# Six attention heads with three dilations: one masked key row per query against a near and a far part

## The chip, the cores and the metric

The program runs on one NeuronCore of a Trainium2 chip. The metric is the device time of one execution in microseconds (us); the median of three executions stands for the kernel. The engines are TensorE (PE, with its weight loads as PEld), VectorE (DVE), ScalarE (ACT), GpSimd (POOL) and SyncE (SP), which issues the DMAs.

## The reference, cut to what matters

A trunk of two layers over 1024 tokens of width 1024, in float32. Each layer is one input projection, three token mixers side by side (retention, dilated attention, spatial gating), an output projection and a SwiGLU. The change touches only the attention of six heads of width 64:

```python
DILATED_PATTERNS = ((128, 1), (512, 4), (2048, 16))
# each pattern: causal attention to t, t-d, ..., t-window; output o and log-denominator lse
w = jax.nn.softmax(jnp.stack(lses, axis=0), axis=0)
return jnp.sum(w[..., None] * jnp.stack(outs, axis=0), axis=0)
```

Mixing the three patterns by their log-denominators is the same as one softmax in which a key that stands in two or three patterns counts two or three times. A query thus sees every key up to 128 tokens back and, farther back, only keys at a distance that is a multiple of 4.

## The kernel before

All matrices are held as two float32r parts (high and low), so that a product is two or three matmuls. A Python scheduler writes the program: coroutines for the attention units, projections and weight loads are advanced against an estimated clock, and `Program.order` then lists the operations of each engine by start in that estimate. On the chip every engine works through its list in order. Copies may be given to ACT or DVE, whichever the scheduler finds freer. DMAs all go through SP's queue in its listed order; a DMA waits there for what it reads and for its semaphore's earlier use.

Buffers come from pools of slots: `U` (128x1024 floats in SBUF, 44), `H` (128x512, 10), `ST` (small statistics, 24), `B` (the 8 PSUM banks).

Attention of one layer: 6 heads, each as 4 units of 256 queries (`att_unit(head, j)`), on 4 lanes that interleave with the projections of gating and retention. A unit makes `qd` (queries high and low), then for each of its two tiles of 128 queries the scores against all earlier keys (`sb_b<-ks_u,qd_h`, up to 1024 columns, high and low), one DVE pass that adds the mask and takes the row maximum (shown as CUSTOM_DVE, in an order as ISA), an exponential on ACT with the row sum, a reciprocal, and a scaling of the whole row (`pr_u<-pr_u,st_st`). PE then transposes the row by blocks of 128 (`tb_b<-cst,pr_u`), ACT or DVE split the transposed block into `ph`/`pl`, and PE multiplies by the values (`ob_b<-ph_h,vs_u`, 256 queries wide). The mask holds the log of the count of patterns:

```python
dist = (NT - 1) * P + i[:, None] - np.arange(S)[None, :]
...
mm(ob[:, i0 * P:256], vs[:, k, :], hi[:, pos:pos + w], k == 0, False)
```

Of the kernel before, what the change touches and what calls it, by code (L numbers as in the profile page):

```python
# [18 lines left out]
P = 128  # L19
# [55 lines left out]
def _constants():  # L75
    c = np.zeros((P, K_END), np.float32)
    i = np.arange(P)
    c[:, K_ID:K_ID + P] = np.eye(P)
    c[:, K_TRIL:K_TRIL + P] = i[:, None] >= i[None, :]
    lg = np.log(1.0 - 2.0 ** (-5.0 - np.arange(6)))  # L80
    diff = (i[None, :] - i[:, None]).astype(np.float64)
    for h in range(6):
        c[:, K_DEC + h * P:K_DEC + (h + 1) * P] = np.where(
            diff >= 0, np.exp(-lg[h] * (i[:, None] + 1.0)) * HD ** -0.5, 0.0)
        c[:, K_ZETA + h] = np.exp(lg[h] * (P - 1.0 - i)) * HD ** -0.5
    for p in range(3):
# [7 lines left out]
    dist = (NT - 1) * P + i[:, None] - np.arange(S)[None, :]  # L94
    count = np.zeros(dist.shape)
    for window, dil in ((128, 1), (512, 4), (2048, 16)):
        count += (dist >= 0) & (dist <= window) & (dist % dil == 0)
    with np.errstate(divide="ignore"):
        mask = np.where(count > 0, HD ** 0.5 * np.log(count), NEG)
    return c, mask.astype(np.float32)  # L100


class Ref:
# [28 lines left out]
    def rearrange(self, pattern, **kw):  # L132

        left, right = (_axes(x)[1:] for x in pattern.split("->"))
        sizes = dict(kw)
        for group, n in zip(left, self.free.shape):
            known = math.prod(sizes[x] for x in group if x in sizes)
            for x in group:
                sizes.setdefault(x, n // known)
        assert sum(left, []) == sum(right, [])  # L140
        return self._with(("rearrange", (pattern,), kw),
                          free=self.free.reshape([math.prod(sizes[x] for x in g) for g in right]))

# [331 lines left out]
def _body(ctx, tc, nc, x, positions, g_mix_pre, g_mix_post, w_in, w_s, b_s, w_out,  # L475
# [9 lines left out]
    U = Slots(u_pool, "u", 44, [P, 1024])  # L485
    H = Slots(u_pool, "h", 10, [P, 512])
    ST = Slots(u_pool, "st", 24, [P, 8])
    O = Slots(u_pool, "o", 2, [P, 256])
# [18 lines left out]
    rvs = fixed([S, 384], "rvs", pool=dram)  # L507
    gs = fixed([HID, S], "gs", pool=dram)
# [756 lines left out]
    def rope_evac(r, hf, b):  # L1265
        z = H.alloc(name="z")
# [14 lines left out]
    att_left = [0]  # L1281

    def att_pair(p, rq, rk, av):

        pair = [8]
        for e in range(2):
            while U.left < 2 + 2:
                yield None
            a, o = slice(e * HD, e * HD + HD), slice(HD - e * HD, 2 * HD - e * HD)
            ks = U.alloc(dtype=F32R, name="ks")  # L1290
            copy(ks[a], rk[a])
            tt(ks[o], rk[a], ks[a].bitcast(F32), ALU.subtract)
            vs = U.alloc([P, NT, P], F32R, "vs")
            copy(vs[:, :, 0:HD], av[:, :, a])
            tt(vs[:, :, HD:P], av[:, :, a], vs[:, :, 0:HD].bitcast(F32), ALU.subtract)
            head = dict(pair=pair, rq=rq, ks=ks, vs=vs, left=4, p=p, e=e)
            for j in range(4):
                att_q.append((head, j))
            yield ()
        U.free(rk, av)  # L1300

    def att_unit(head, j):
# [5 lines left out]
        while H.left < 3:  # L1308
            yield None
        qd = H.alloc([P, 2, 256], F32R, "qd")  # L1310
        rj = rq[a, j * 256:j * 256 + 256]
        copy(qd[a, 0, :], rj)
        copy(qd[o, 0, :], rj)
        tt(qd[a, 1, :], rj, qd[a, 0, :].bitcast(F32), ALU.subtract)
        copy(qd[o, 1, :], qd[a, 1, :].bitcast(F32))
        yield (qd[:],)
        while U.left < (2 if 3 + p in yT else 3):
            yield None
        if 3 + p not in yT:
            yT[3 + p] = U.alloc(name="yT")  # L1320
            y_left[3 + p] = 8
        pr = [U.alloc(name="pr"), U.alloc(name="pr")]
        for i in range(2):
            t = 2 * j + i
            n = (t + 1) * P
            off = (NT - 1 - t) * P
            st = ST.alloc(name="st")
            nch = (n + 511) // 512
            while B.left < nch + 1:
                yield None  # L1330

            cut = [0, n] if nch == 1 else [0, min(512, n - 256), n]
            for c in range(nch):
                c0, c1 = cut[c:c + 2]
                b = B.alloc(name="sb")
                for v in range(2):
                    mm(b[:, 0:c1 - c0], qd[:, v, i * P:(i + 1) * P], ks[:, c0:c1], v == 0, v == 1)
                sm, mx, ms = pr[i][:, c0:c1], st[:, c:c + 1], L["mask"][:, off + c0:off + c1]
                prog.add(dict(dve=(1.042 * (c1 - c0) + 80, nc.vector.tensor_tensor_reduce)),
                         [sm, mx], [b[:, 0:c1 - c0], ms], out=sm, in0=b[:, 0:c1 - c0], in1=ms, scale=1.0,  # L1340
                         scalar=-3.0e38, op0=ALU.add, op1=ALU.max, accum_out=mx)
                B.free(b)
            if nch == 2:
                tt(st[:, 0:1], st[:, 0:1], st[:, 1:2], ALU.max)
            ts(st[:, 2:3], st[:, 0:1], -HD ** -0.5, ALU.mult)
            act(pr[i][:, 0:n], pr[i][:, 0:n], AF.Exp, scale=HD ** -0.5, bias=st[:, 2:3], accum_out=st[:, 3:4])
            prog.add(dict(dve=(75.0, nc.vector.reciprocal)), [st[:, 4:5]], [st[:, 3:4]],
                     out=st[:, 4:5], in_=st[:, 3:4])
            scaled(pr[i][:, 0:n], pr[i][:, 0:n], st[:, 4:5])
            ST.free(st)  # L1350
            yield ()
        H.free(qd)
        yield (pr[0][:], pr[1][:])
        while B.left < 4 or H.left < 3:
            yield None
        ob = B.alloc(name="ob")
        pend = None
        nb = 2 * j + 2
        for g in range(j + 2):
            new = None  # L1360
            if g <= j:
                while B.left < 2 or H.left < 3:
                    yield None
                b = B.alloc(name="tb")
                pos, lay = 0, []
                for k in (2 * g, 2 * g + 1):
                    i0 = 0 if k <= 2 * j else 1
                    for i in range(i0, 2):
                        tr(b[:, pos + (i - i0) * P:pos + (i - i0 + 1) * P], pr[i][:, k * P:(k + 1) * P])
                    lay.append((k, i0, pos))  # L1370
                    pos += (2 - i0) * P
                hi = H.alloc(dtype=F32R, name="ph")
                lo = H.alloc(dtype=F32R, name="pl")
                copy(hi[:, 0:pos], b[:, 0:pos])
                tt(lo[:, 0:pos], b[:, 0:pos], hi[:, 0:pos].bitcast(F32), ALU.subtract)
                B.free(b)
                new = (hi, lo, lay)
            if pend is not None:
                hi, lo, lay = pend
                for k, i0, pos in lay:  # L1380
                    w = (2 - i0) * P
                    mm(ob[:, i0 * P:256], vs[:, k, :], hi[:, pos:pos + w], k == 0, False)
                    mm(ob[:, i0 * P:256], vs[:, k, :], lo[:, pos:pos + w], False, k == nb - 1)
# [4 lines left out]
        U.free(*pr)  # L1388
        tmp = O.alloc(name="ot")
        y = yT[3 + p]  # L1390
        copy(tmp[0:HD, :], ob[HD:P, 0:256])
        tt(y[a, j * 256:j * 256 + 256], ob[0:HD, 0:256], tmp[0:HD, :], ALU.add)
        B.free(ob)
        O.free(tmp)
        head["left"] -= 1
        head["pair"][0] -= 1
        if head["left"] == 0:
            U.free(ks, vs)
# [13 lines left out]
    def gnorm(src, dst):  # L1412
# [3 lines left out]
        reduce(st[:], src)  # L1416
        ts(st[:], st[:], -1.0 / HD, ALU.mult)
        tt(dst, src, st[:].unsqueeze(2).to_broadcast([P, 8, HD]), ALU.add)
        act(sq[:], dst, AF.Square)
        reduce(st[:], sq[:])  # L1420
        rstd(st[:], HD, 8)
        tt(dst, dst, st[:].unsqueeze(2).to_broadcast([P, 8, HD]), ALU.mult)
# [149 lines left out]
    def layer(l):  # L1572
# [5 lines left out]
        room(3)  # L1578
        av = [U.alloc([P, NT, P], F32, "av") for _ in range(3)]

        def ev_a(t, b):
            for p in range(3):
                copy(av[p][:, t, :], b[:, p * P:(p + 1) * P])
# [15 lines left out]
        dma(L["mask"][:], amask)  # L1599
        sch.spawn(load_ws(l))  # L1600
        att_left[0] = 24
        for _ in range(LANES):
            sch.spawn(att_lane())
        for p in range(3):
# [5 lines left out]
            sch.spawn(att_pair(p, r[0], r[1], av[p]), r[1][:])  # L1610
# [5 lines left out]
        def ev_g(t, b):  # L1616
            for q in range(2):
                act(vg[q][:, t, :], b[:, q * P:(q + 1) * P], AF.Gelu_apprx_tanh)
            if t % 4 == 3:
                for q in range(2):  # L1620
# [13 lines left out]
        def ev_r(t, b):  # L1634
            v = H.alloc([P, 384], F32, "v")
# [125 lines left out]
    if VERBOSE:  # L1761
        print("slots left at the tightest:", {s.tag: s.low for s in (U, H, ST, B, O)},
# [24 lines left out]
```

## Time and profile before

| | |
|---|---|
| time, median of 3 runs | 2313.69 us (2310.02 to 2316.12) |
| profiled execution | 2311.72 us, of which span 2309.9 us |
| PE, PEld busy | 2280.2 us (99%), 1930.3 us (84%) |
| DVE, ACT, POOL busy | 1772.0 us (77%), 886.4 us (38%), 83.1 us (4%) |
| DMA | 225.61 MB, mean 98 GB/s |
| mean granted clock of TensorE | 0.998 of full speed |

The busy time of PE counts each matmul from its start to a modelled end, and matmuls overlap; what a matmul costs the stream is read from the start of one to the start of the next. Attention stands in the profile between about 97 and 322 us and, for the second layer, between about 1239 and 1464 us.

### The profile page before, as it was taken

The page shows a single profiled execution, that of the slowest core. Times are in us where ns is not written, and L with a number is a line of the kernel's source. Part 1 is how long each engine was busy: PE and PEld are TensorE (multiplying, and loading weights), DVE is VectorE, ACT ScalarE, POOL GpSimd, SP SyncE. Part 2 cuts the span into 40 slices and gives each one's busy share as a digit, 9 for nine tenths or more (in the row PEclk, how much of TensorE's full clock was granted, in tenths as well). Part 3 has the DMA queues.
Part 4 walks back from the last instruction along what each step waited for, and adds up shares of the span by engine and source line. Part 5 has one row for each costly group of instructions (what it writes and reads, how often), then busy time and mean ns, then how long its engine had stood idle before and what let it go on. Part 6 is the DMA issues. An engine that isn't in the chain of part 4 may idle for free. (4 is left out here: it accounts for less than half of the span.)

```text
span 2309.9 us, 30253 instructions
## 1 busy us (share of the span) xinstructions
PE 2280.2 (99%) x11320; PEld 1930.3 (84%) x11320; DVE 1772.0 (77%) x3265; ACT 886.4 (38%) x1625; POOL 83.1 (4%) x95
## 2 busy tenths in 40 slices
PE   8999999999999999999999999999999999999998
PEld 7898988887888888878898898888878888888786
DVE  7698876688985554889957898766989755549896
ACT  5367532344122222434344674221632222225441
POOL 1000001010000000000100100000100000000000
PEclk9999999999999999999999999999999999999999
DMA  6211132242432223422342112231623322253142
GB/s 192 78 40 37 58 83 69 96 144 76 133 105 86 84 85 124 177 106 75 132 150 60 32 44 74 77 92 55 193 76 114 101 83 82 82 181 148 55 134 94
DMA packets 213058, 225.61 MB, mean 98 GB/s; under 512 B 14000, under 2 KB 170800, under 8 KB 212912
## 3 DMA queue, kind: packets, MB, share of 16 engines
q1 hardware_dynamic: 212912, 223.69, 30.9%
q8 instruction: 89, 1.46, 0.3%
q14 instruction: 57, 0.47, 0.1%
HBM read 167.01 MB, written 44.04 MB: 91 GB/s over the span
## 5 line engine op out<-in xcount | busy, mean ns | idle before, releaser
L583 PE MATMUL w_b<-hs_u,wh_u 128*128 128x512 f32 x1280 | 394.9, 390 | 2.3 <-DVE wh_u L1760 1.9
L583 PE MATMUL db_b<-wb_u,ga_u 128*128 128x512 f32 x1512 | 347.0, 391 | 2.9 <-DVE ga_u L543 2.6
L583 PE MATMUL fb_b<-hT_u,wh_u 128*128 128x512 f32 x1088 | 344.4, 397 | 0.0
L583 PEld LDWEIGHTS db_b<-wb_u,ga_u 128*128 128x128 f32 x1512 | 284.5, 188 | 65.1 <-DVE ga_u L543 4.1
L583 PEld LDWEIGHTS w_b<-hs_u,wh_u 128*128 128x128 f32 x1280 | 239.7, 188 | 54.2 <-DVE wh_u L1760 2.7
L583 PE MATMUL w_b<-hT_u,wh_u 128*128 128x512 f32 x832 | 257.6, 390 | 0.0
L583 PE MATMUL w_b<-hs_u,wl_u 128*128 128x512 f32 x640 | 248.8, 390 | 1.1 <-DVE wl_u L543 1.1
L583 PEld LDWEIGHTS fb_b<-hT_u,wh_u 128*128 128x128 f32 x1088 | 196.9, 188 | 36.5 <-issue 1.0
L583 PE MATMUL fb_b<-hT_u,wl_u 128*128 128x512 f32 x544 | 212.9, 391 | 0.0
L543 DVE TENSOR_TENSOR c_h<-w_b,c_h 128x512 f32<-128x512 f32 x192 | 131.4, 687 | 80.5 <-PE w_b L583 79.0
L583 PE MATMUL pb_b<-wh_u,hT_u 128*128 128x384 f32 (+1 forms) x768 | 191.0, 324 | 0.0
L543 DVE TENSOR_TENSOR f_u<-f_u,db_b 128x512 f32<-128x512 f32 x232 | 152.2, 684 | 46.7 <-PE db_b L583 46.5
L583 PEld LDWEIGHTS w_b<-hT_u,wh_u 128*128 128x128 f32 x832 | 155.7, 188 | 32.0
L583 PE MATMUL w_b<-hT_u,wl_u 128*128 128x512 f32 x416 | 161.6, 389 | 0.0
L543 DVE TENSOR_TENSOR wl_u<-wr_u,wh_u 128x1024 fp32r<-128x1024 f32 (+1 forms) x130 | 152.6, 1186 | 1.4 <-ACT wh_u L532 0.9
L583 PEld LDWEIGHTS w_b<-hs_u,wl_u 128*128 128x128 f32 x640 | 120.1, 188 | 27.5 <-DVE wl_u L543 2.5
L583 PEld LDWEIGHTS pb_b<-wh_u,hT_u 128*128 128x128 f32 x768 | 134.6, 190 | 1.4 <-ACT hT_u L532 0.3
L583 PE MATMUL pb_b<-wl_u,hT_u 128*128 128x384 f32 (+1 forms) x384 | 122.6, 319 | 0.3 <-DVE wl_u L543 0.3
L583 PEld LDWEIGHTS fb_b<-hT_u,wl_u 128*128 128x128 f32 x544 | 102.1, 188 | 21.8
L532 ACT ACTIVATE wh_u<-wr_u 128x1024 fp32r<-128x1024 f32 (+1 forms) x83 | 84.8, 1037 | 81.8 <-DVE ws_u L543 54.9
L532 ACT ACTIVATE c_h<-w_b 128x512 f32<-128x512 f32 x82 | 49.1, 599 | 165.1 <-PE w_b L583 165.1
L543 DVE TENSOR_TENSOR wl_u<-ws_u,wh_u 128x1024 fp32r<-128x1024 f32 x88 | 106.8, 1217 | 0.1
(198 smaller groups left out, 4059.3 us busy)
## 6 DMA issues: line engine op xcount, KB each, us to landing
wr_u<-w_gate_up SPq DMA_DIRECT2D x176, 256.0 KB, 3.8
gs<-c_h SPq DMA_DIRECT2D x88, 256.0 KB, 2.3
wr_u<-gs SPq DMA_DIRECT2D x44, 512.0 KB, 7.0
wr_u<-w_down SPq DMA_DIRECT2D x44, 512.0 KB, 5.5
wr_u<-w_in SPq DMA_DIRECT2D x38, 512.0 KB, 4.4
sw_h<-z_h SPq DMA_DIRECT2D x192, 64.0 KB, 2.0
wr_u<-w_out SPq DMA_DIRECT2D x16, 512.0 KB, 3.8
wr_u<-w_gate_up SPq DMA_DIRECT2D x16, 512.0 KB, 4.8
```

Of the source, the lines that this page charges most:

```text
L532: alts = dict(act=(act_cost(o, a), lambda out, in_: nc.scalar.activation(out=out, in_=in_, func=AF.Copy)), dve=(1.042 * o.size + 68 if a.r ...
L543: lambda out, in0, in1: nc.vector.tensor_tensor(out=out, in0=in0, in1=in1, op=op))
L583: prog.add(dict(pe=(cost + 3, lambda out, lhsT, rhs: nc.tensor.matmul(out, lhsT, rhs, start=start, stop=stop, skip_group_check=on_top))), ...
```

## The change

A unit is now 512 queries of a head (`att_unit(head, h)`, 2 per head). Its keys are in two parts. The near part: each tile of 128 queries against its own and the previous 128 keys. The far part: queries are regrouped by token mod 4, and each of the 4 groups of 128 queries meets the keys of the same residue, 128 (h = 0) or 256 (h = 1) of them, with keys that the near part has masked out. For that, queries and keys are read with a step of 4 tokens by TensorE. Each part has its own maximum and sum, per query, in different partitions; each part stores them to a DRAM tensor `exch` and loads the other's, and `att_factors` makes the scale from both. Values are stored to DRAM once (`avs`) and loaded in both token orders. The near part's transposed blocks are regrouped by residue as they are split, so that both parts add up in one PSUM bank `ob`. The DMA scratch of the program is set to 1024 bytes, and `U` has 47 slots, `H` 11; `ST` has 20 of twice the width.

```diff
+    dist = P + i[:, None] - np.arange(2 * P)[None, :]
+    dist = np.concatenate([np.where(dist <= P, dist, -1), np.where(4 * dist > P, 4 * dist, -1)], 1)
...
+    def att_factors(x):
+        y = ST.alloc(name="sf")
+        xv = x[:].rearrange("p (w k c) -> p w k c", w=2, k=2)
+        e = y[:, 4:12].rearrange("p (w c) -> p w c", w=2)
+        tt(y[:, 0:4], x[:, 0:4], x[:, 8:12], ALU.max)
+        tt(e, xv[:, :, 0], y[:, 0:4].unsqueeze(1).to_broadcast([P, 2, 4]), ALU.subtract)
+        act(y[:, 4:12], y[:, 4:12], AF.Exp, scale=HD ** -0.5)
+        tt(xv[:, :, 1], xv[:, :, 1], e, ALU.mult)
+        tt(y[:, 0:4], x[:, 4:8], x[:, 12:16], ALU.add)
...
+        tt(y[:, 12:16], y[:, 4:8], y[:, 0:4], ALU.mult)
...
+                if part == 0:
+                    t = 4 * h + c
+                    n = 256 if t else P
+                    ql = [q[:, c * P:(c + 1) * P] for q in (q_hi, q_lo)]
+                    kr = ks[:, (t + 1) * P - n:(t + 1) * P]
...
+                else:
+                    n = w
+                    per = 512 // n
+                    ql = [q[:].rearrange("p (i c) -> p i c", c=4)[:, :, c] for q in (q_hi, q_lo)]
+                    kr = ks[:, 0:4 * n].rearrange("p (i c) -> p i c", c=4)[:, :, c]
...
+                for v in range(2):
+                    mm(bs, ql[v], kr, v == 0, v == 1)
...
+        views = [("k (c q) -> q k c", dict(q=P)), ("k (q c) -> q k c", dict(q=P))]
...
+        for i, x in enumerate(stats):
+            dma(stored(i, i), x[:, 0:8].rearrange("p (k c) -> p k c", k=2))
+        for i, x in enumerate(stats):
+            dma(x[:, 8:16].rearrange("p (k c) -> p k c", k=2), stored(i, 1 - i))
+        yield (stats[0][:], stats[1][:])
+        fs = [att_factors(x) for x in stats]
...
+        obv = ob[:].rearrange("p (c a b) -> p c a b", c=4, b=32).swap("p c a b -> p a c b", 1, 0, 2)
...
+        fars = [([far[:, c, k * P:(k + 1) * P]], vs[1][:, 4 * k + c, :], ob[:, c * P:(c + 1) * P])
+                for k in range(h + 1) for c in range(4)]
...
+                if g < 2:
+                    src = src.rearrange("p n (i c) -> p n i c", c=4).swap("p n i c -> p n c i", 0, 2, 1)
+                    hv, lv = (x.rearrange("p n (c i) -> p n c i", c=4) for x in (hv, lv))
+                copy(hv, src)
+                tt(lv, src, hv.bitcast(F32), ALU.subtract)
...
-    nc = bacc.Bacc("TRN2", target_bir_lowering=False, num_devices=1)
+    nc = bacc.Bacc("TRN2", target_bir_lowering=False, num_devices=1, dynamic_dma_scratch_size=1024)
```

Matmuls of the attention in the order of both layers, those of all other names being unchanged in number and shape:

| columns | before | after |
|---|---|---|
| scores `sb` 512, 384, 256, 128 | 120, 72, 72, 24 | 0, 0, 264, 120 |
| of these read with a step of 4 tokens | none | 96 of 256, 96 of 128 |
| transposes `tb<-pr` 128 | 432 | 324 |
| values `ob` 256, 128 | 384, 96 | 144, 360 |

First place, PE's list in the first attention stretch of layer 0, value products of a unit (`fb`, `pb` are projections). Before:

```order
L583 MATMUL ob_b_1185<-ph_h_1082,vs_u_639 128x256
L583 MATMUL ob_b_1185<-pl_h_1106,vs_u_639 128x256
L583 MATMUL ob_b_1185<-ph_h_1082,vs_u_639 128x128
L583 MATMUL ob_b_1185<-pl_h_1106,vs_u_639 128x128
L593 MATMUL tb_b_1192<-cst,pr_u_999 128x128
```

Of the change:

```order
L590 MATMUL ob_b_1391<-ph_h_1394,vs_u_698 128x2x4x32
L590 MATMUL ob_b_1391<-pl_h_1408,vs_u_698 128x2x4x32
L590 MATMUL ob_b_1391<-ph_h_1394,vs_u_698 128x4x32
L590 MATMUL ob_b_1391<-pl_h_1408,vs_u_698 128x4x32
L600 MATMUL tb_b_1444<-cst,pr_u_1062 128x128 x4
```

Products 256 columns wide remain for the near part only; the far part's are 128 wide.

Second place, DVE's list of the change behind the masks of the unit whose tiles are `pr_u_2475` (near) and `pr_u_2496` (far); before, a reciprocal stood there on its own:

```order
L1855 COPY v_h_2597<-pb_b_2510 128x384
L550 TENSOR_TENSOR sf_st_2633<-st_st_2476 128x4
L550 TENSOR_TENSOR sf_st_2633<-st_st_2476,sf_st_2633 128x8
L1855 COPY v_h_2640<-pb_b_2593 128x384
L550 TENSOR_TENSOR st_st_2476<-st_st_2476,sf_st_2633 128x2x4
L550 TENSOR_TENSOR sf_st_2633<-st_st_2476 128x4
L1855 RECIPROCAL sf_st_2633<-sf_st_2633 128x4
```

Between them now stand emptyings of PSUM banks of the projection (`v_h<-pb_b`), which wait behind the first `sf_st` in this list.

Third place, SP's list of the change for the same unit; before, only the `rvs` stores and weight loads stood here:

```order
L1855 DMA rvs<-v_h_2505 128x384
L1855 DMA exch<-st_st_2497 128x2x4
L1855 DMA rvs<-v_h_2597 128x384
L1855 DMA exch<-st_st_2476 128x8x1
L1855 DMA st_st_2476<-exch 128x8x1
L1855 DMA exch<-st_st_2561 128x2x4
L1855 DMA st_st_2497<-exch 128x2x4
L1855 DMA rvs<-v_h_2640 128x384
```

Each load of `exch` stands behind the store that it waits for, and stores of the projection behind both.

## Rows read from the trace of the kernel before

**Rows 1.** The page, busy time of PE and weight loads: us (share) x instructions.

```profile
PE 2280.2 (99%) x11320; PEld 1930.3 (84%) x11320; DVE 1772.0 (77%) x3265; ACT 886.4 (38%) x1625; POOL 83.1 (4%) x95
```

**Rows 2.** Windows: busy us of PE, PEld, DVE, ACT, POOL in the attention stretch.

```profile
97.00:322.00 225.00, 223.61 (x1380) 200.69 (x1379) 197.12 (x545) 136.08 (x277) 8.45 (x6) 1.00 0.20 57
```

**Rows 3.** Waits of PE, whole span: us, times, longest.

```profile
PE tb_b L593 <- DVE pr_u L561: 1.4, 2, 0.7
PE ob_b L583 <- DVE pl_h L543: 1.0, 3, 0.4
```

**Rows 4.** Groups by shape, PE, attention: xcount | busy us, mean ns of one.

```profile
L593 PE MATMUL tb_b<-cst,pr_u 128*128 128x128 f32 x432 | 68.8, 273 | 1.6 <-DVE pr_u L561 1.4
L583 PE MATMUL ob_b<-ph_h,vs_u 128*128 128x256 f32 x192 | 57.3, 315 | 0.0
...
L583 PE MATMUL sb_b<-ks_u,qd_h 128*128 128x512 f32 x120 | 36.1, 398 | 0.0
...
L583 PE MATMUL sb_b<-ks_u,qd_h 128*128 128x384 f32 x72 | 18.6, 344 | 0.0
...
L583 PE MATMUL sb_b<-ks_u,qd_h 128*128 128x256 f32 x72 | 15.1, 296 | 0.0
```

**Rows 5.** Timeline of PE: start us, us, matmuls of 512, 256 and 128 columns.

```profile
115.88 0.39 PE L583 MATMUL fb_b<-hT_u,wl_u 128*128 128x512 f32 x1
116.11 0.28 PE L583 MATMUL ob_b<-ph_h,vs_u 128*128 128x256 f32 x1
116.22 0.28 PE L583 MATMUL ob_b<-pl_h,vs_u 128*128 128x256 f32 x1
116.34 0.22 PE L583 MATMUL ob_b<-ph_h,vs_u 128*128 128x128 f32 x1
116.40 0.28 PE L583 MATMUL ob_b<-pl_h,vs_u 128*128 128x128 f32 x1
116.52 0.52 PE L593 MATMUL tb_b<-cst,pr_u 128*128 128x128 f32 x3
```

**Rows 6.** Timeline of PE, matmuls of 384 columns.

```profile
220.66 0.51 PE L583 MATMUL pb_b<-wh_u,hT_u 128*128 128x384 f32 x2
221.01 0.34 PE L583 MATMUL pb_b<-wl_u,hT_u 128*128 128x384 f32 x1
```

**Rows 7.** Timeline of PE, four transposes and the two matmuls behind them.

```profile
109.03 0.60 PE L593 MATMUL tb_b<-cst,pr_u 128*128 128x128 f32 x4
109.38 0.71 PE L583 MATMUL fb_b<-hT_u,wh_u 128*128 128x512 f32 x2
109.93 0.40 PE L583 MATMUL fb_b<-hT_u,wl_u 128*128 128x512 f32 x1
```

**Rows 8.** Timeline of PE, a plain float32 matmul whose columns come in runs of 64.

```profile
180.70 1.02 PE L583 MATMUL mb_b<-vg_u,wsT 128*128 128x512 f32 x2
181.15 1.03 PE L583 MATMUL fb_b<-hT_u,wh_u 128*128 128x512 f32 x2
182.02 0.40 PE L583 MATMUL fb_b<-hT_u,wl_u 128*128 128x512 f32 x1
```

**Rows 9.** Tile `bs_c` (512 elements of 4 bytes a load), issue to landing us.

```profile
DMA to landing us min/median/max: 2.1/3.9/5.7
```

**Rows 10.** DMA issues: xcount, KB each, us to landing (1024 elements of 4 bytes).

```profile
pi_st<-positions SPq DMA_DIRECT2D x1, 4.0 KB, 9.7
```

**Rows 11.** Groups by shape, DVE and ACT: xcount | busy us, mean ns of one.

```profile
L543 DVE TENSOR_TENSOR pl_h<-tb_b,ph_h 128x384 fp32r<-128x384 f32 x48 | 26.3, 548 | 0.9 <-ACT ph_h L532 0.7
...
L1760 DVE CUSTOM_DVE_ANT_0 pr_u<-sb_b,mask_u 128x256 f32<-128x256 f32 x36 | 15.0, 416 | 0.1
...
L1760 DVE RECIPROCAL st_st<-st_st 128x1 f32<-128x1 f32 x96 | 14.2, 156 | 10.2 <-ACT pr_u L527 9.7
...
L527 ACT ACT_TABLE_LOAD x30 | 38.5, 1283 | 7.3 <-DVE st_st L553 5.8 <-PEq L1775 0.7
...
L527 ACT ACTIVATION_READ_ACCUMULATOR pr_u<-pr_u,st_st 128x1 f32 x96 | 18.0, 187 | 0.0
...
L527 ACT ACTIVATE pr_u<-pr_u,st_st 128x256 f32<-128x256 f32 x12 | 6.0, 496 | 0.0
```

More of the change, by code (lines that the diff above doesn't have):

```diff
@@ L507, in _body @@
     rvs = fixed([S, 384], "rvs", pool=dram)
+    avs = fixed([S, 384], "avs", pool=dram)
+    exch = fixed([4 * 12 * DEPTH, 512], "exch", pool=dram)
     gs = fixed([HID, S], "gs", pool=dram)
@@ L1265, in rope_evac @@
     def rope_evac(r, hf, b):
+        sch.until(lambda: H.left >= 2)
         z = H.alloc(name="z")
@@ L1281, in _body, with att_pair @@
     att_left = [0]
-    def att_pair(p, rq, rk, av):
-        pair = [8]
+    att_ctr = [0]
+    def att_pair(p, rq, rk):
+        pair = [4]
         for e in range(2):
-            while U.left < 2 + 2:
+            while U.left < 4:
                 yield None
             a, o = slice(e * HD, e * HD + HD), slice(HD - e * HD, 2 * HD - e * HD)
+            raw = U.alloc([P, 2, NT, HD], F32, "av")
+            src = avs[:, p * P + e * HD:p * P + e * HD + HD]
+            dma(raw[:, 0], by_tile(src))
+            for h in range(2):
+                dma(raw[:, 1, 4 * h:4 * h + 4], src[h * 512:h * 512 + 512]._with(
+                    ("rearrange", ("(i c) d -> i c d",), dict(c=4))))
             ks = U.alloc(dtype=F32R, name="ks")
@@ L1292, in att_pair, with att_unit @@
             tt(ks[o], rk[a], ks[a].bitcast(F32), ALU.subtract)
[L1293 to L1298, printed above, removed]
-            yield ()
-        U.free(rk, av)
-    def att_unit(head, j):
+            vs = [U.alloc([P, NT, P], F32R, "vs") for _ in range(2)]
+            for v, i in zip(vs, range(2)):
+                copy(v[:, :, 0:HD], raw[:, i])
+                tt(v[:, :, HD:P], raw[:, i], v[:, :, 0:HD].bitcast(F32), ALU.subtract)
+            U.free(raw)
+            head = dict(pair=pair, rq=rq, ks=ks, vs=vs, left=2, p=p, e=e)
+            for h in range(2):
+                att_q.append((head, h))
+            yield ()
+        U.free(rk)
+    def att_factors(x):
[7 more added lines that the diff above has]
+        tt(y[:, 0:4], x[:, 4:8], x[:, 12:16], ALU.add)
+        prog.add(dict(dve=(75.0, nc.vector.reciprocal)), [y[:, 0:4]], [y[:, 0:4]], out=y[:, 0:4], in_=y[:, 0:4])
+        tt(y[:, 12:16], y[:, 4:8], y[:, 0:4], ALU.mult)
+        ST.free(x)
+        return y
+    def att_unit(head, h):
         p, e = head["p"], head["e"]
@@ L1307, in att_unit @@
         yield (ks[:],)
-        while H.left < 3:
+        while H.left < 6:
             yield None
[L1310 to L1316, printed above, removed]
+        q_hi, q_lo = (H.alloc(dtype=F32R, name="qd") for _ in range(2))
+        rj = rq[a, h * 512:h * 512 + 512]
+        copy(q_hi[a], rj)
+        copy(q_hi[o], rj)
+        tt(q_lo[a], rj, q_hi[a].bitcast(F32), ALU.subtract)
+        copy(q_lo[o], q_lo[a].bitcast(F32))
+        yield (q_lo[:],)
         while U.left < (2 if 3 + p in yT else 3):
@@ L1320, in att_unit @@
             yT[3 + p] = U.alloc(name="yT")
[L1321 to L1335, printed above, removed]
-                for v in range(2):
[L1337 to L1350, printed above, removed]
-            yield ()
@@ new lines, in att_unit, with stored @@
+        H.free(q_hi, q_lo)
+        u = 4 * att_ctr[0]
+        att_ctr[0] += 1
+        rows = [exch[u + 2 * i:u + 2 * i + 2, :] for i in range(2)]
+        views = [("k (c q) -> q k c", dict(q=P)), ("k (q c) -> q k c", dict(q=P))]
+        def stored(i, j):
+            return rows[j]._with(("rearrange", (views[i][0],), views[i][1]))
+        for i, x in enumerate(stats):
+            dma(stored(i, i), x[:, 0:8].rearrange("p (k c) -> p k c", k=2))
+        for i, x in enumerate(stats):
+            dma(x[:, 8:16].rearrange("p (k c) -> p k c", k=2), stored(i, 1 - i))
@@ L1355, in att_unit @@
+        yield (stats[0][:], stats[1][:])
+        fs = [att_factors(x) for x in stats]
+        for c in range(4):
+            v = near[:, c, (0 if h or c else P):256]
+            scaled(v, v, fs[0][:, 12 + c:13 + c])
+        for c in range(4):
+            v = far[:, c, 0:w]
+            scaled(v, v, fs[1][:, 12 + c:13 + c])
+        ST.free(*fs)
+        yield (near[:], far[:])
+        while B.left < 4 or H.left < 6:
             yield None
         ob = B.alloc(name="ob")
+        obv = ob[:].rearrange("p (c a b) -> p c a b", c=4, b=32).swap("p c a b -> p a c b", 1, 0, 2)
@@ new lines, in att_unit @@
+        near_of = lambda c, k: near[:, c, k * P:(k + 1) * P]
+        banks = [[([near_of(c, 1), near_of(c + 1, 0)], vs[0][:, 4 * h + c, :], obv[:, c:c + 2])
+                  for c in (0, 2)]]
+        last = [([near_of(1, 1), near_of(2, 0)], vs[0][:, 4 * h + 1, :], obv[:, 1:3]),
+                ([near_of(3, 1)], vs[0][:, 4 * h + 3, :], obv[:, 3:4])]
+        if h:
+            last.append(([near_of(0, 0)], vs[0][:, 3, :], obv[:, 0:1]))
+        banks.append(last)
+        fars = [([far[:, c, k * P:(k + 1) * P]], vs[1][:, 4 * k + c, :], ob[:, c * P:(c + 1) * P])
+                for k in range(h + 1) for c in range(4)]
@@ L1357, in att_unit @@
+        banks += [fars[i:i + 4] for i in range(0, len(fars), 4)]
         pend = None
-        nb = 2 * j + 2
-        for g in range(j + 2):
+        for g in range(len(banks) + 1):
             new = None
-            if g <= j:
-                while B.left < 2 or H.left < 3:
+            if g < len(banks):
+                while B.left < 2 or H.left < (2 if pend else 6):
                     yield None
@@ L1379, in att_unit @@
                 hi, lo, lay = pend
[L1380 to L1383, printed above, removed]
+                for q, (v, out_, pos, n) in enumerate(lay):
+                    first = g == 1 and q == 0
+                    mm(out_, v, hi[:, pos:pos + n], first, True, not first)
+                    mm(out_, v, lo[:, pos:pos + n], False, True, True)
                 H.free(hi, lo)
@@ L1575, in layer @@
         y_left.clear()
-        room(3)
-        av = [U.alloc([P, NT, P], F32, "av") for _ in range(3)]
         def ev_a(t, b):
-            for p in range(3):
-                copy(av[p][:, t, :], b[:, p * P:(p + 1) * P])
+            sch.until(lambda: H.left >= 1)
+            v = H.alloc([P, 384], F32, "v")
+            copy(v[:], b[:, 0:384])
+            dma(avs[t * P:(t + 1) * P, :], v[:])
+            H.free(v)
         def tables(t):
@@ L1619, in ev_g @@
             if t % 4 == 3:
+                sch.until(lambda: H.left >= 1)
                 for q in range(2):
@@ L1761, in _body @@
     if VERBOSE:
-        print("slots left at the tightest:", {s.tag: s.low for s in (U, H, ST, B, O)},
+        print("slots left at the tightest:", {s.tag: s.low for s in (U, H, ST, B)},
               "clock", {k: round(v / 1e3, 1) for k, v in prog.t.items()}, "ordered", round(total / 1e3, 1))
```

91 lines of the change are left out of this document (60 added, 31 removed).

## The prediction

> **What bounds the kernel now.** I read the page's busy times first: PE works 99% of the span, the next engine, DVE, 77% [rows 1]. So the time is the length of PE's list plus what it waits, and a change counts by the matmuls it takes out of the list or puts in, and by new waits. The window over the attention stretch comes second, because an average of 77% can hide a full engine: there DVE is busy 197.1 of 225 us (28 idle), ACT 136.1 (89 idle), PE 223.6, and the granted clock is full [rows 2]. Third, the list of who waited: PE waits for the scaled scores `pr_u` 1.4 us and for the split blocks `pl_h` 1.0 us in the whole span [rows 3]. Attention today hides everything but its own matmuls. The groups by shape give their counts [rows 4], of which the mean of one is a latency and no price; the price is the distance between starts in the timeline [rows 5 to 8].
>
> **What the matmuls cost, before and after.** From start to start: 512 columns 0.23 us (115.88 to 116.11); 256 columns 0.115 (116.11 to 116.34 is two); 128 columns 0.06 when it follows a longer one, and 0.12 when it follows another 128, as long as a 256, because its weights come too late to be hidden [rows 5]. 384 columns: 0.35 for two, 0.175 [rows 6]. Four transposes and two 512s take 0.90 us, less 0.46 leaves 0.11 for a transpose [rows 7]. With the counts of the order (before: both layers, in the table of the change):
>
> Before: scores 120 x 0.23 + 72 x 0.175 + 72 x 0.115 + 12 pairs of 128 at 0.18 = 50.7; values 384 x 0.115 + 48 pairs x 0.18 = 52.8; transposes 432 x 0.11 = 47.5. Sum 151.0 us.
>
> After: scores 264 x 0.115 + 12 pairs x 0.18 + 12 runs of eight 128s at 0.06 + 7 x 0.12 = 0.90, together 43.4. Values 144 x 0.115 = 16.6, 36 runs of eight at 0.90 = 32.4, and the near part's 12 pairs and 12 runs of four (0.42) = 7.2, together 56.2. Transposes 324 x 0.11 = 35.6. Sum 135.2 us.
>
> PE's list is 15.8 us shorter. The gain is small beside the keys left out because the far part works 128 wide, where a matmul costs as much as one of 256: the values even cost 3.4 us more.
>
> **Reading with a step of four.** 192 of the far scores take queries as weights and keys as moving columns with a step of four tokens, 16 bytes. Nothing in the trace reads TensorE's operands so. From below: full rate, nothing added; no gain is possible, since the 0.115 is already what 256 contiguous columns take. From above the slowest column of the trace, the plain float32 matmul whose moving columns come in runs of 64: 180.70 to 182.02 less two 512s (0.46) is 0.86 us for 512, 1.68 ns a column [rows 8]. At that, 256 columns take 0.43 (+0.315 x 96 = 30 us) and 128 take 0.215 against 0.1125 (+0.10 x 96 = 10 us): 40 us in all. Between them lies the rate at which weights come in single columns, 0.12 us for 128 [rows 5], 0.94 ns a column: 256 would take 0.24 (+0.125 x 96 = 12 us), and the 128s are paced by it already. [...] Both ends stay for the range.
>
> [...]
>
> **The work on DVE and ACT.** DVE's mask passes go from 144 to 192 with a quarter fewer columns, about even. Small operations go from 240 (reciprocals, maxima, negations) to 336, at 0.16 us [rows 11] 15 us more; 36 subtractions of 384 columns fall away at 0.55, 20 us less [rows 11]. So DVE has no more to do than before and is covered by its 28 us idle a layer. If that cover shrinks: the 48 near blocks are read from PSUM with a step of four by two passes each; were each longer by another 0.55 us, that is 53 us over two engines and two layers, 13 for each engine in a stretch, still under 28 and 89. ACT reads 96 more row sums (x 0.187 = 18 us) and loads 8 more tables (x 1.283 = 10 us) [rows 11]; 14 us a layer against 89 idle. I count both at nothing.
>
> **The exchange.** A unit stores maxima and sums of both parts and loads them back: two landings in a row, 96 DMAs, and each load stands in SP's list behind its store. What is queued behind: on SP the `rvs` stores, weight loads and `sw_h` swaps; on DVE, behind the first `sf_st`, emptyings of `pb` banks on which PE's next projection tile rests. PE is spared as long as its list holds other matmuls between a unit's last far score and its first near transpose. I counted them. For the unit in the places shown it is 81 of 384 columns, 6 of 256, 10 of 128 and 4 transposes: 14.2 + 0.7 + 1.2 + 0.4 = 16.5 us. The twelve gaps of a layer are 16.2, 16.5, 18.9, 20.0, 20.6, 21.5 and longer, to 31.8 us. The chain that must fit: the last two masks 0.8, eight exponentials with their row sums 8 x 0.68 = 5.5, two landings, five small operations 0.8, a table load 1.3, two scalings at most 0.8 [rows 11]: 9.2 us and the landings. The nearest landing is `bs_c`, single elements of 4 bytes: 2.1 us at its fastest, 5.7 at its slowest [rows 9]; `pi_st`, of 1024 elements like half of the exchange, took 9.7 among the first loads of the program [rows 10]. In the attention stretch the DMA engines are busy 20% [rows 2], so I take 2.1: 13.4 us fit into 16.2, and the exchange costs nothing.
>
> The 36 loads of `avs` and 16 stores stand in SP's list well ahead of their use, and the additional slots can shorten only the waits of PE, 2.4 us [rows 3]: nothing for both.
>
> **Sum.** -15.8 + 12 = about -4 us. The profiled execution took 2311.7 us (span 2309.9 and 1.8 around it), the median of the runs is 2.0 above it. 2311.7 - 4 + 2 = 2310 us.
>
> **The rivals.** *Full rate.* The step costs TensorE nothing: 2313.7 - 15.8 = 2298 us. For it: a float32r column is one element wherever it lies. Against it: the faster an engine takes its columns, the less time there is for each address, and a 256 runs at 0.45 ns a column, the fastest of all reads here.
>
> *Slow columns.* The step costs what the slowest row shows: -15.8 + 40 = +24, 2338 us. It decides against the change from 16 us for the 192 matmuls, that is from about 0.28 us for a 256 with the 128s unchanged. For it: the row exists, and nothing shows a faster read of single columns by the moving side. [...]
>
> *The exchange comes late.* At 5.7 us a landing the chain is 20.6 us, later than four gaps by 4.4, 4.1, 1.7 and 0.6, 10.8 us a layer; PE stands at `tb_b<-cst,pr_u` for 22 us: 2332. It decides from two landings of 7.0 us together. For it: 1024 single elements a transfer, half of them written to DRAM, which no row shows, and loads of weights before them in the same queue. Against it: the quiet 2.1 us, and a 20% busy share. [...]
>
> **How the numbers follow.** The bound for faster or slower is 0.3% of the median, 6.9 us, about what a measurement of this kernel tells from no change. Chances: my forecast 0.35, full rate 0.22, slow columns 0.25, exchange late 0.18. My forecast alone spans 2303 to 2316 (the column cost between 0.18 and 0.28 us): faster in 0.08 of its 0.35, same in 0.25, slower in 0.02. With full rate, faster has 0.30; the exchange at its mildest gives same another 0.02; slower has 0.43. The range goes from 2296, just under full rate, to 2344, above slow columns by as much as their 128s may be dearer still; outside are late landings like the 9.7.
>
> **What would show it.** The starts of `sb_b<-ks_u,qd_h` of 256 columns in the runs of eight: 0.115, 0.24 or 0.43 us apart, and of 128: 0.12 or 0.2. The landings of `exch<-st_st` and `st_st<-exch` around 2 us, and DVE's waits for them; the waits of PE at `tb_b<-cst,pr_u` as small as now. Transposes still at 0.11, values of 128 at 0.12 in a run. I am wrong if DVE is busy clearly above 197 us in the stretch, or if PE waits for anything of attention by more than 3 us a layer.

## The result, and the profile after

The changed kernel takes 2469.06 us in the median of 4 runs (2466.0 to 2472.47), the kernel before 2312.48 beside it: a ratio of 1.0676, 95% interval 1.0655 to 1.0697. It is slower by 157 us, where 2310 was forecast and the range ended at 2344.

The page of the changed kernel: busy time of PE and PEld, then the granted clock of TensorE in 40 slices (tenths of full speed, 9 is 90% or more).

```profile
PE 2324.8 (94%) x11332; PEld 1974.1 (80%) x11332; DVE 1762.7 (71%) x3409; ACT 922.8 (37%) x1793; POOL 82.5 (3%) x95
PEclk9988889999999999999999889899999999999999
```

Against [rows 1], PE's share falls from 99% to 94%, and DVE has 9 us less to do than before: no engine has become the bound, PE waits. The windows over the stretch of [rows 2], then two pieces of the first layer's attention, which is longer here (its exchange runs from 110 to 380 us); columns as in [rows 2].

```profile
97.00:322.00 225.00, 182.90 (x1050) 166.43 (x1049) 139.03 (x457) 113.08 (x274) 7.14 (x4) 0.89 0.26 43
200.00:250.00 50.00, 34.15 (x181) 26.60 (x180) 33.60 (x92) 32.85 (x56) 7.14 (x4) 0.83 0.28 45
350.00:407.00 57.00, 42.32 (x223) 35.60 (x222) 35.57 (x96) 20.98 (x48) 0.96 (x1) 0.82 0.39 70
```

In the same 225 us PE is busy 182.9 instead of 223.6, at a clock of 0.89 instead of 1.00. What it waits for stands in the list of PE's waits, here with DVE's two and SP's one on the exchange (us in total, times, longest).

```profile
PE tb_b L600 <- DVE pr_u L568: 64.3, 17, 8.2
PE pb_b L590 <- DVE wh_u L1855: 31.1, 2, 15.6
PE tb_b L600 <- ACT pr_u L566: 14.4, 2, 7.8
...
DVE sf_st L550 <- DMA st_st<-exch: 132.7, 29, 12.2
DVE st_st L550 <- DMA exch<-st_st: 47.8, 8, 7.8
...
SPq L1855 <- DMA exch<-st_st: 165.9, 32, 10.6
```

PE's wait for `pr_u`, 1.4 us in [rows 3], is now 78.7, and 31.1 us go to weights (`wh_u`) for `pb`. Behind both stands the exchange. The DMA issues (count, KB each, median us to landing, over the 32 stores and 33 loads whose landing can be told), and pieces of the chain that ended last (start us, us):

```profile
exch<-st_st SPq DMA_DIRECT2D x48, 4.0 KB, 9.9
st_st<-exch SPq DMA_DIRECT2D x48, 4.0 KB, 3.3
```

```profile
1490.82 10.71 DMA st_st<-exch
1503.28 10.54 DMA exch<-st_st
1513.91 0.18 DVE st_st L550
...
1566.12 17.88 DMA exch<-st_st
1584.09 0.17 DVE st_st L550
```

Two landings in a row take 13 us by the medians and nearly 20 at the longest; 4.2 were forecast. Behind the two stores of these pieces the chain has no load but `st_st`, which multiplies a part's own sums in place: DVE holds it back until the store of these sums has landed (the 47.8 us above). A wait also has a price behind it. The timeline of PE (start us, us), after a wait of 8.17 us:

```profile
222.50 0.45 PE L600 MATMUL tb_b<-cst,pr_u 128*128 128x128 f32 x1 [8.17 <-DVE pr_u L568]
...
225.98 1.02 PE L590 MATMUL fb_b<-hT_u,wh_u 128*128 128x512 f32 x2
226.83 0.40 PE L590 MATMUL fb_b<-hT_u,wl_u 128*128 128x512 f32 x1
227.12 0.36 PE L590 MATMUL ob_b<-ph_h,vs_u 128*128 128x256 f32 x1
```

The window over it, columns as in [rows 2]:

```profile
222.50:226.80 4.30, 3.93 (x14) 3.19 (x15) 4.22 (x12) 2.02 (x3) 2.85 (x2) 0.50 0.20 33
```

The two 512s from 225.98 to 226.83 take 0.43 us each, against 0.23 before: the granted clock of this window is 0.50, against 1.00 in [rows 2]. The 512 behind them takes 0.29.

By stages, from the first `fb_b` to the first `w_b` the first layer takes 86.1 us more (545.6 for 459.6), and the second, from the end of the first layer to its first `w_b`, 84.1 more; the four SwiGLU stretches take 13.5 less.

### The profile page after: what moved, and what is told of

The parts are those of the page before. It is cut to its first block, busy times and chain, and to the rows that moved or that the text cites. A ratio compares the mean times of both kernels' runs of the same rounds, so it can differ in the third digit from the quotient of the medians.

```text
span 2467.6 us, 30797 instructions
## 1 busy us (share of the span) xinstructions
PE 2324.8 (94%) x11332; PEld 1974.1 (80%) x11332; DVE 1762.7 (71%) x3409; ACT 922.8 (37%) x1793; POOL 82.5 (3%) x95
## 2 busy tenths in 40 slices
DMA packets 303494, 234.96 MB, mean 95 GB/s; under 512 B 102384, under 2 KB 261232, under 8 KB 303344
## 3 DMA queue, kind: packets, MB, share of 16 engines
q1 hardware_dynamic: 303344, 233.00, 33.2%
## 5 line engine op out<-in xcount | busy, mean ns | idle before, releaser
L590 PE MATMUL fb_b<-hT_u,wh_u 128*128 128x512 f32 x1088 | 355.9, 408 | 0.0
L590 PEld LDWEIGHTS fb_b<-hT_u,wh_u 128*128 128x128 f32 x1088 | 207.0, 196 | 41.4 <-issue 1.9
L590 PE MATMUL pb_b<-wh_u,hT_u 128*128 128x384 f32 (+1 forms) x768 | 199.9, 334 | 31.9 <-DVE wh_u L1855 31.1
L590 PE MATMUL fb_b<-hT_u,wl_u 128*128 128x512 f32 x544 | 218.6, 402 | 0.0
L590 PEld LDWEIGHTS pb_b<-wh_u,hT_u 128*128 128x128 f32 x768 | 141.9, 199 | 33.8 <-DVE wh_u L1855 32.3
L600 PE MATMUL tb_b<-cst,pr_u 128*128 128x128 f32 x324 | 67.0, 320 | 79.0 <-DVE pr_u L568 64.3
L539 ACT ACTIVATE wh_u<-wr_u 128x1024 fp32r<-128x1024 f32 (+1 forms) x93 | 94.4, 1030 | 102.7 <-DVE wl_u L550 64.4
L539 ACT ACTIVATE wh_u<-ws_u 128x1024 fp32r<-128x1024 f32 x74 | 78.6, 1062 | 117.5 <-DVE ws_u L550 106.6
```

The lines of the kernel that those rows point to most:

```text
L539: alts = dict(act=(act_cost(o, a), lambda out, in_: nc.scalar.activation(out=out, in_=in_, func=AF.Copy)), dve=(1.042 * o.size + 68 if a.r ...
L590: prog.add(dict(pe=(cost + 3, lambda out, lhsT, rhs: nc.tensor.matmul(out, lhsT, rhs, start=start, stop=stop, skip_group_check=on_top))), ...
L600: prog.add(dict(pe=(109.0, lambda out, in_, identity: nc.tensor.transpose(out, in_, identity))), [o], [i, ident], out=o, in_=i, identity=i ...
```

## The experiments

Theory A: the factors wait for two late landings. Theory B: the exchange's DMAs hold SP's queue, and weights and swaps behind them are late. Theory C: the two parts' own work on DVE, ACT and PE is too much. Where a ratio is given, it is to the kernel before on the same chip, whose medians were 2311.7 to 2312.2 us.

**No exchange.** In `att_factors` the other part's columns are replaced by the part's own, and the DMAs are left out of the program after the scheduler has placed them (the `False` below), so the order of all else is that of the change.

```diff
-        tt(y[:, 0:4], x[:, 0:4], x[:, 8:12], ALU.max)
+        tt(y[:, 0:4], x[:, 0:4], x[:, 8:12], ALU.max, only=(x[:, 0:4], x[:, 0:4]))
...
-            dma(stored(i, i), x[:, 0:8].rearrange("p (k c) -> p k c", k=2))
+            dma(stored(i, i), x[:, 0:8].rearrange("p (k c) -> p k c", k=2), False)
...
```

> The order of every engine is that of the change, but the 96 DMAs of the exchange are not issued and the factors are made from the part's own maxima and sums (so the two parts are not brought to a common scale). Theory A, the landings: the factors wait for two landings in a row, about 10 and 2 to 10 us, and PE runs out of other work; theory B, the queue: the exchange's DMAs hold SP's queue and the weight loads behind it come late. Both expect PE's waits, 133 us in the changed kernel, to fall under 10, the granted clock to go back to 1.0 and a time of 2313.7 - 15.8 (shorter list) + 23 (256s and 128s of the far scores at 0.234 us) - 13.6 (SwiGLU stages, as the changed kernel ran them) = 2307 us, 2298 to 2318. Theory C, the parts' own work on DVE and ACT: above 2380 us, with waits for pr_u left.

Measured: 2308.59 us, ratio 0.9984 (0.9975 to 0.9994). PE's waits fall to 15.4 us in the whole span, with none for `pr_u`, and the mean clock is 0.998 (0.97 in the change). The exchange costs 160.5 us, and theory C falls. Of the 160.5, 117 are PE's waits (132.9 less 15.4). The other 43 stand in PE's busy time, 2324.8 us in the change for as many matmuls; the page of this run:

```profile
PE 2281.5 (99%) x11332; PEld 1943.8 (84%) x11332; DVE 1760.1 (76%) x3409; ACT 922.0 (40%) x1793; POOL 83.6 (4%) x95
```

I put these 43 down to matmuls at the lower clock behind such waits, as those above; that is argued from the rows and has no run of its own.

**The exchange issued, and read by nobody.** The same factors from own columns, with all 96 DMAs in their places. Here, as in the run without exchange, the product of the sums goes to columns that no store reads.

> As without exchange, but its 96 DMAs are issued in their places of SP's queue, and what they bring is read by nobody (the two parts are not brought to a common scale). Theory A, the landings: the wait of DVE for st_st<-exch is what costs, so that the time stays within 20 us of the run without exchange, 2307 to 2327 us, and PE waits for pr_u under 10 us. Theory B, the queue: loads of exch still wait for their stores in SP's queue, weight loads behind them are late, and PE waits for wh_u by 30 us or more, 2400 us or above. In between, both have a share.

Measured: 2423.57 us, ratio 1.0491 (1.0473 to 1.0509). So 115 us are lost without anybody waiting for the other part's numbers, and 45.5 more when these are read and the own sums are overwritten: DVE's waits of 132.7 and 47.8 us are both gone here, and no run parts the two. PE waits 32.1 us for `wh_u`, as B expects, but also 45.9 us for `pr_u`, where A expected under 10, and DVE waits 94.3 us for the swaps `sw_h`, in the change 31.7. PE's longest wait of either kind ends just behind a wait of DVE for a swap. The timelines of DVE and of PE:

```profile
149.77 0.69 DVE L550 TENSOR_TENSOR sw_h<-sw_h,tab_u 128x512 f32<-128x512 f32 x1 [4.97 <-DMA sw_h<-z_h]
...
332.29 0.69 DVE L550 TENSOR_TENSOR sw_h<-sw_h,tab_u 128x512 f32<-128x512 f32 x1 [13.36 <-DMA sw_h<-z_h]
```

```profile
151.12 0.58 PE L591 MATMUL pb_b<-wh_u,hT_u 128*128 128x256 f32 x1 [17.18 <-DVE wh_u L1857]
...
333.30 0.47 PE L601 MATMUL tb_b<-cst,pr_u 128*128 128x128 f32 x1 [12.96 <-DVE pr_u L569]
```

In both places PE waits through DVE's list, in which `wh_u` and `pr_u` stand behind the swaps. The late swaps could come from SP's list, or from the transfers themselves.

**Unlinked loads.** The loads read a constant of the same row length, so no load in SP's queue waits for a store.

```diff
-            dma(x[:, 8:16].rearrange("p (k c) -> p k c", k=2), stored(i, 1 - i))
+            dma(x[:, 8:16].rearrange("p (k c) -> p k c", k=2), stored(i, 1 - i),
+                amask[0:2, :].rearrange(views[i][0], **views[i][1]))
```

> As the exchange that is read by nobody (2423.6 us), but the loads come from a constant in DRAM of the same shape of rows, so that in SP's queue no load waits for a store; stores, loads and their single elements are as many. If it is the wait in SP's list, and what stands behind it, that made the exchange cost 115 us unread: the time falls to that without exchange, 2308 to 2320 us, and the swaps of sw_h land in time (DVE's wait for them 94 back to about 32 us). If the stores hold the DMA engines themselves, so that swaps and weights behind them land late whoever waits in the queue: 2380 to 2425 us.

Measured: 2409.70 us, ratio 1.0417 (1.0399 to 1.0436). SP's wait for its own stores, 173.7 us in the run before and 24.1 here, was worth 14 us of the time; the other 101 stay, so the place that theory B names, loads that wait in SP's list, is the lesser part. The list of what waits for `sw_h`, how long its issues take (ns: min, median, max) and its landings (us: min, median, max, over the 95 of 192 that can be told):

```profile
DVE sw_h L551 <- DMA sw_h<-z_h: 88.6, 24, 11.6
```

```profile
L1859 SPq DMA_DIRECT2D sw_h<-z_h x192: 507/588/6387, 62.4 to 1646.6; - x192
DMA to landing us min/median/max: 1.9/2.0/15.2
```

A swap of 64 KB that lands in 2.0 us at the median needs up to 15.2; in the kernel before its longest is 3.8. The stores hold up other transfers, though the DMA engines are busy only 31% between 95 and 420 us of this run. Part of it still happens on SP: the issue of a swap itself takes up to 6.4 us here, against 1.9 in the kernel before.

**Elements 64 bytes apart.** As unlinked, but the near part's 1024 elements of a store are put 64 bytes apart in DRAM; count, size and order stay (303344 packets of SP's queue in both runs).

```diff
-            dma(stored(i, i), x[:, 0:8].rearrange("p (k c) -> p k c", k=2))
+            far_apart = exchw[u // 4:u // 4 + 1, :]._with(
+                ("rearrange", ("r (k c q x) -> (r q) (k c) x",), dict(k=2, c=4, x=16)))._with(
+                ("__getitem__", ((slice(None), slice(None), slice(0, 1)),), {}))
+            dma(stored(i, i), x[:, 0:8].rearrange("p (k c) -> p k c", k=2), to=None if i else far_apart)
...
```

> As the exchange with unlinked loads (2409.7 us), and the near part's 1024 single elements of a store go 64 bytes apart in DRAM in place of side by side (and nobody reads them). If single elements are slow because neighbours meet in one line of memory: they land in 2 to 4 us and the time is 2310 to 2330. If each small store is slow wherever it goes: landings of 9 us or more and 2400 to 2415 us.

Measured: 2310.41 us, ratio 0.9992 (0.9982 to 1.0001). 99 us are gone by the addresses alone. The DMA issues of this run, and the landings of its swaps:

```profile
exch<-st_st SPq DMA_DIRECT2D x24, 4.0 KB, 2.5
exchw<-st_st SPq DMA_DIRECT2D x24, 4.0 KB, 3.2
```

```profile
DMA to landing us min/median/max: 1.9/2.0/4.4
```

The single elements land in 3.2 us (2.6 to 6.0 over the 24); side by side, where their landing can be told (11 of 24), they took 9.4 to 19.5 in the run before this one. So neither the size of the pieces nor their number alone makes them late; it takes single elements stored next to each other. No other distance than 64 bytes was tried.

**The change with this one thing altered.** The near part's elements 64 bytes apart, and read; nothing is left out, and the far part needs two loads for one.

```diff
-        for i, x in enumerate(stats):
-            dma(stored(i, i), x[:, 0:8].rearrange("p (k c) -> p k c", k=2))
+        dma(apart("r (k c q x) -> (r q) (k c) x", every, every, slice(0, 1), k=2, c=4, x=16),
+            stats[0][:, 0:8].unsqueeze(2))
+        dma(stored(1, 1), stats[1][:, 0:8].rearrange("p (k c) -> p k c", k=2))
...
```

> The change itself, with one thing altered: the near part's maxima and sums, still single elements, lie 64 bytes apart in DRAM (and the far part fetches them in two loads of 512 elements for one of 1024, since they no longer lie side by side). If the neighbours in a line were the whole cause: stores land in 3 to 4 us, swaps in 2 to 4, PE waits for pr_u fall from 79 us to under 10, and the time is that without exchange plus what the remaining landings show, as in the whole stores (10 us): 2309 to 2325 us. If reading the exchange has a cost of its own, the 46 us between the change and the same exchange unread: 2340 to 2360.

Measured: 2328.87 us, ratio 1.0069 (1.0052 to 1.0086), a little above the upper end of what the neighbours alone should leave. Stores land in 3.5 us, loads in 2.9 to 3.4, swaps in 3.9 at the longest, and PE waits 7.9 us for `pr_u`. 140 of the 160.5 us came from the neighbours; 20 remain. PE's waits are 28.0 us in the whole span, 12.6 more than without exchange, in many small pieces; which landing makes them was not tried.

**Whole stores.** Maxima and sums side by side in SBUF (`p (w c k)`), so that each store writes 32 bytes a partition, and each load takes pieces of 8 bytes.

> The change with maxima and sums side by side, so that each store writes 32 bytes a partition in one piece (128 pieces) and each load takes pieces of 8 bytes (512 a unit and part, the far part's in four DMAs of 32 partitions). If single-element stores to DRAM are what lands late: stores and loads land in 2 to 3 us, the chain is 9.2 + 5 = 14.2 us and fits before the shortest gap of 16, PE's waits fall under 20 us, time 2305 to 2330 us. If small pieces are slow whichever way they go: loads stay at 5 to 10 us, PE's waits at half or more, time 2360 to 2430 us. Theory C: no change, about 2469 us.

Measured: 2319.22 us, ratio 1.0034 (1.0021 to 1.0047). The DMA issues:

```profile
st_st<-exch SPq DMA_DIRECT2D x96, 1.0 KB, 2.0
exch<-st_st SPq DMA_DIRECT2D x48, 4.0 KB, 1.6
st_st<-exch SPq DMA_DIRECT2D x24, 4.0 KB, 2.0
```

Loads of small pieces are quick here; it was the stores that were slow. The exchange then costs 10.6 us, and the change is still no gain.

**Pieces of 8 bytes.** The near part stores 512 pieces of 8 bytes side by side, and the far part loads whole rows.

> The change with the near part's store in pieces of 8 bytes (512 for 1024) and its far load whole; the far part stores whole and is loaded by pieces of 8. If a store costs by its pieces: 5 to 6 us to land against 10.2, and about half of the time lost to the exchange stays, 2360 to 2400 us. If stores of 8 bytes go as quickly as 16 and 32 (1.5 to 2 us): 2305 to 2325 us. If whatever is under some size takes the full 10 us: 2440 to 2475.

Measured: 2329.60 us, ratio 1.0076 (1.0061 to 1.0091), between the first two cases. These stores land in 4.5 us (3.1 to 7.3): as the first case has it, about half of 10.2, but the time lost is 21 us and not half. I take it that the gaps cover such a landing: 9.2 us of chain, 4.5 and 2.4 for a load make 16.1, and the shortest gap was 16.2. That is argued and was not tried.

**A scheduler that knows of the late landing.** Each store to `exch` costs 8 us more in the scheduler's estimate.

> The change, with the scheduler's estimate of each store to exch raised by 8 us (about what they took), nothing else; the result is the same. If an order that knows of the late landing can hide it: loads stand later in SP's list, behind other work, factors later in DVE's, PE's waits for pr_u fall from 79 us to under 30, time 2330 to 2400 us. If the stores themselves hold the DMA engines, or a unit's work cannot be spread so far: 2420 to 2470 us.

Measured: 2454.64 us, ratio 1.0619 (1.06 to 1.0638), 14 us better than the change. PE's waits move from weights to factors:

```profile
PE tb_b L602 <- DVE pr_u L570: 112.8, 10, 18.1
...
PE pb_b L592 <- DVE wh_u L1857: 1.6, 2, 0.8
```

The weights are in time now and the factors later; DVE waits 64.6 us for swaps, in the change 31.7. This order did not hide the stores. Few of their landings can be told (10 of 48, 2.2 to 14.5 us).

**What the step of four costs.** Without exchange, the far scores take 128 queries side by side as weights:

```diff
-                    ql = [q[:].rearrange("p (i c) -> p i c", c=4)[:, :, c] for q in (q_hi, q_lo)]
+                    ql = [q[:, c * P:(c + 1) * P] for q in (q_hi, q_lo)]
```

> As without exchange (2308.6 us), and the far scores take their weights from 128 queries side by side in place of every fourth (so they are scores of other queries); keys still move with a step of four tokens. If the step costs in the weight load: far 256s at 0.117 us and far 128s at 0.11 in a run, 96 x 0.117 + 96 x 0.12 = 23 us less, 2286 us. If it costs in the moving keys: both stay at 0.234 us and the time at 2306 to 2311. If the 256s alone stay at 0.234 (keys) while the 128s fall (weights): about 2297.

and then the keys side by side too (`kr = ks[:, c * n:(c + 1) * n]`):

> As without exchange and with plain weights (2296.1 us, far 128s at 0.118 us, far 256s still at 0.233), and the far keys side by side too. Far 256s fall to 0.117 us: 96 x 0.116 = 11 us less, 2285 us, if a moving column costs 0.91 ns with the step and 0.46 without; then the forecast's shorter list (15.8 us) and the slots (10.4) account for the time before less this one, 2312 - 26 = 2286. If the 256s stay at 0.233 (the bank, or the run of equal widths): 2296.

Measured: 2296.07 us, ratio 0.9934 (0.9917 to 0.9952), and 2286.52, ratio 0.9888 (0.9873 to 0.9902). The timeline of PE over one run of 40 scores, among them 8 far ones of 128 columns and 8 of 256: without exchange, with plain weights, with both plain.

```profile
101.80 6.85 PE L591 MATMUL sb_b<-ks_u,qd_h 128*128 128x128 f32 x40
108.49 0.63 PE L591 MATMUL fb_b<-hT_u,wh_u 128*128 128x512 f32 x2
```

```profile
102.15 5.81 PE L591 MATMUL sb_b<-ks_u,qd_h 128*128 128x128 f32 x40
107.80 0.63 PE L591 MATMUL fb_b<-hT_u,wh_u 128*128 128x512 f32 x2
```

```profile
103.13 4.83 PE L591 MATMUL sb_b<-ks_u,qd_h 128*128 128x128 f32 x40
107.80 0.63 PE L591 MATMUL fb_b<-hT_u,wh_u 128*128 128x512 f32 x2
```

From start to start 6.69, 5.65 and 4.67 us: each plain side takes 1.0 us off, 0.12 to 0.13 a matmul. It is the third of the cases expected for plain weights: the weights set the 128s (0.234 with the step, 0.118 without), the keys still hold the 256s at 0.233 when the weights are plain, and 0.12 with both plain.

**Regrouped queries.** Whole stores, and `qd` copied once a unit into two more tiles in residue order.

> The change with whole stores (2319.2 us), and the queries regrouped once a unit into two more tiles of H, so that the far scores' weights lie side by side: 96 copies of 128x512 more, about 0.42 us on DVE or 0.62 on ACT, 20 to 30 us a layer over two engines that have room. If the step costs in the weight load: 23 us less, 2290 to 2302 us, faster than the kernel before by 0.4 to 0.9%. If the copies come in the way of the stages that feed PE: 2305 to 2320. If the step costs in the moving keys: 2319 or more.

Measured: 2333.11 us, ratio 1.009 (1.0074 to 1.0106), 14 us slower than the whole stores, where the weights alone should give 12.5 back. The copies are 48 and not 96, but dearer than said (groups by shape: count, busy us, mean ns):

```profile
L1860 DVE CAST qd_h<-qd_h 128x512 fp32r<-128x512 f32 x24 | 14.8, 624 | 0.1
...
L539 ACT ACTIVATE qd_h<-qd_h 128x512 fp32r<-128x512 f32 x24 | 27.4, 1144 | 3.1 <-DVE qd_h L1860 2.1 <-PE sb_b L590 0.7
```

A unit also waits for 8 of the 11 slots of `H` where it waited for 6. Which of the two delays PE was not tried.

**The pools alone.** The kernel before with the small scratch, `U` 47 and `H` 11.

> The kernel before with the DMA scratch at 1024 bytes and 47 slots of U and 11 of H, nothing else. In the changed kernel the stages of the SwiGLU are 13.6 us shorter in sum. If the slots do it: 2313.7 - 13.6 = 2300 us, 2296 to 2305. If it comes from what else changed in the order: 2310 to 2316 us.

Measured: 2301.33 us, ratio 0.9957 (0.9942 to 0.9972): the part of the change that pays, faster than both kernels and the fastest version here that leaves nothing out. The windows over the two SwiGLU stretches of the first layer, before and with the pools:

```profile
513.00:939.00 426.00, 423.85 (x1882) 349.64 (x1881) 290.07 (x405) 124.11 (x183) 5.11 (x5) 1.00 0.36 111
939.00:1160.00 221.00, 219.50 (x981) 180.83 (x980) 208.99 (x344) 98.35 (x175) 6.54 (x12) 1.00 0.30 108
```

```profile
514.00:937.00 423.00, 423.00 (x1883) 350.31 (x1882) 292.77 (x412) 132.84 (x187) 3.65 (x5) 1.00 0.38 118
937.00:1156.00 219.00, 219.00 (x983) 181.49 (x982) 208.93 (x346) 94.53 (x165) 6.55 (x12) 1.00 0.28 99
```

PE is busy without a break there with the pools; before, it stood for 3.7 us in both together.

## Why the prediction was wrong

The terms as they measured, on the 2312 us of before: list and slots -25.5 (2286.5 with both sides plain), step +22.1 (to 2308.6), exchange +160.5 (to 2469.1).

- **The exchange, counted at nothing: the step that failed.** "In the attention stretch the DMA engines are busy 20% [rows 2], so I take 2.1" took the landing of a quiet load, `bs_c`, for one of 1024 single elements stored side by side. Those took 8.4 to 17.9 us in the change, 10.2 at the median of the 19 whose landing can be told (of 24). That `pi_st`, which the prediction set aside, took 9.7 is no better guide: it is a load, and loads of 1024 single elements landed in 3.4 us at the median where the stores did not hold them up (the change with one thing altered). A busy share told nothing: it rises only to 26%. The rival "the exchange comes late" had the mechanism and the place, `tb_b<-cst,pr_u`, and the point from which it decides, 7.0 us for two landings. At 5.7 us a landing it gave 22 us and not 160, and it left out what is larger: of the 160.5, 101 is other transfers, the swaps above all, held up by these stores, 14 is SP's wait for its own stores, and 45.5 is what reading adds: the wait for the factors, which alone was priced, and DVE's wait until sums that it overwrites are stored, which the prediction does not have. (In the order of the runs: unlinked, unread, change.)
- **What is queued behind.** The prediction named the `rvs` stores, weight loads and `sw_h` swaps behind the exchange on SP, and priced none of them.
- **The matmul list, -15.8 us: right.** With plain operands and the slots' 10.4 us, 2312 should become 2285.9; measured 2286.5.
- **Reading with a step of four, +12: half of it.** The 256s are right (0.24 forecast, 0.234 measured; 9.6 us). "The 128s are paced by it already" is wrong: a weight load with the step takes 0.234 us and not 0.12, 12.5 us more. The middle of the three rates was the right choice, but it holds for each operand, and weights start from the slower one. The amount is about a factor of two for each operand: 0.234 us for 0.118 in a 128 by the weights, 0.233 for 0.12 in a 256 by the keys.
- **The slots, counted at nothing: -10.4 us.** The 2.4 us of [rows 3] are attention's waits, not all of PE's; the whole list holds 19.7. The waits that the slots shorten stand in the SwiGLU, which the prediction left aside. That 2310 and the 2308.6 without exchange agree is thus chance: +10 and -10 cancel.
- **DVE and ACT, values and transposes: right.** DVE is less busy than before, and without exchange PE waits for none of the regrouped blocks by more than 0.8 us in all.

## What to carry to other kernels

Price a small DMA by its direction and its addresses on both sides, not by its bytes: single elements stored side by side in DRAM landed three times as late as the same elements 64 bytes apart (10.2 us at the median against 3.2), and delayed swaps behind them (17.1 us to land at the longest, 3.8 before). An operation that overwrites what such a store reads waits for it too (47.8 us of DVE in the change). Where two layouts must meet, let the store write whole pieces and the load pick the elements (1.6 and 2.0 us to land in the median). Before counting freed memory at nothing, read the waits of all stages, not those of the stage that is changed.

## What the hardware showed unexpectedly

- Stores of 1024 single elements of 4 bytes side by side: 8.4 to 17.9 us to land in the change; 64 bytes apart 2.6 to 6.0; 512 pieces of 8 bytes side by side 3.1 to 7.3; 128 pieces of 32 bytes 1.4 to 3.0. Loads of 1024 single elements from DRAM: 2.1 us at the quickest. By size alone the first two would be alike; their addresses part them. What the memory does with neighbours no run shows.
- While such stores are under way, swaps of 64 KB land up to 17.1 us after the start of their issue in the change, against 3.8 before, and the issue alone takes up to 8.4 of it, against 1.9.
- A float32r operand read with a step of 16 bytes: weights 1.83 ns a column, for at most 0.92 side by side (the 0.118 us of a 128 while the keys still had the step), moving columns 0.91 for 0.46. The two do not add up: a 256 with both takes 0.234 us, with one 0.233.
- A matmul's output with runs of 32 columns in PSUM cost nothing to be seen: the matmul behind the near part's second product of 256 starts 0.119 us after it in the median (run without exchange), 0.118 before.
